# Rotary embedding on one core: stores moved from the ScalarE queue into the sync queue, and five TensorE tiles in place of three

## The chip, the core and the metric

The kernel runs on 1 core of one Trainium2 chip. The metric is device time in microseconds, the median of several executions. The engines in this text are TensorE (PE in the profile; PEld is its weight load), VectorE (DVE), ScalarE (ACT), GpSimd (POOL) and SyncE (SP), whose work here is to issue transfers. The 16 DMA engines of the core move all data between HBM and the on-chip memory SBUF; q1 is the queue fed by SP, q10 the one fed by ScalarE.

## The reference

```python
# x: (8, 2048, 8, 64) float32;  cos, sin: (2048, 32) float32
def reference(x, cos, sin):
    x1, x2 = x[..., :32], x[..., 32:]
    cos = cos[None, :, None, :]
    sin = sin[None, :, None, :]
    out1 = x1 * cos - x2 * sin
    out2 = x1 * sin + x2 * cos
    return np.concatenate([out1, out2], axis=-1)
```

Every element of x is read once (33.6 MB), and as much is written. The tables are small (0.26 MB each).

## The kernel before

**Slabs.** The sequence is cut into two groups of 1024 positions; in a group each of 128 partitions takes 8 consecutive positions. A slab is one batch and one group: 128 partitions x 4096 floats, 2 MB, 16 KB in one piece for each partition. There are 16 slabs, numbered 0 to 15; slabs 0 to 7 use the tables of group 0, slabs 8 to 15 those of group 1. A slab is loaded into a tile `xt` (nine of them, `NBUF`), rotated in place and stored from there, so load i + 9 has to wait until store i has landed.

**Rotation.** `rotate(i, lo, n)` works on a piece of a slab, in general a half (`UNIT`, 2048 floats per partition); the first half of slab 0 and the last half of slab 15 are cut once more. A piece has one of three kinds:

- kind A, the usual one: GpSimd makes `t2` in two instructions (L151), one half of the pairs times sin, the other times -sin; VectorE makes `t1 = x * cos` (L157) and then `x = t1 + t2` (L164).
- kind B: as A, but the add is done by TensorE: for each 512 columns a matmul of `t1` with the identity and one of `t2` with the identity add up in PSUM (L169, L170), and ScalarE copies the sum back to `xt` (L171).
- kind C: GpSimd does nothing; VectorE makes `x * cos` (L157) and `x * sin` (L174), TensorE adds them with the identity or its negative (L185, L186), and ScalarE copies (L189).

Before, three pieces are not of kind A: the second half of slab 5 (B), and both halves of slab 9 (C and B). `t2` has three buffers, and so has `t1s`, the SBUF tile of kinds B and C.

**Order.** The program is unrolled and handed to a scheduler; `keep(...)` fixes an instruction's place in its engine's program order, what isn't kept may be moved. Before, the DVE, ACT and store instructions are kept; loads and GpSimd's multiplications are not. The two halves of slab 0's first half therefore stand on GpSimd as sin, sin, -sin, -sin.

**Transfers.** Loads and tables are issued by SP (L82, L83, L89), stores by ScalarE (L196), where they stand in line with ScalarE's copies from PSUM and its table work (`prepare`). Store i - 2 is issued after slab i (`LAG = 2`), the last three after one another at the end. The nine first loads are at the head of SP's queue; load i + 6 comes after slab i.

Of the kernel before, what the change touches and what calls it, by code (L numbers as in the profile page):

```python
# [9 lines left out]
@with_exitstack  # L10
def kernel(
    ctx: ExitStack,
    tc: tile.TileContext,
    x: bass.AP,
    cos: bass.AP,
    sin: bass.AP,
    out: bass.AP,
):
    nc = tc.nc
    keep = tc.keep_in_program_order  # L20
    f32 = mybir.dt.float32
    PSUM = bass.MemoryType.PSUM

    B, S, H, D = x.shape
    Dh = D // 2
    P = 128
    HD = H * D
    R = S // P

    SL = 8  # L30
    n_half = R // SL
    SLAB = SL * HD
    UNIT = 4 * HD
    NBUF = 9
    C = 512

    xv = x.rearrange("b (g q r) h d -> b g q (r h d)", q=P, r=SL)
    ov = out.rearrange("b (g q r) h d -> b g q (r h d)", q=P, r=SL)
    cos_src = cos.rearrange("(g q r) d -> g q r d", q=P, r=SL)
    sin_src = sin.rearrange("(g q r) d -> g q r d", q=P, r=SL)  # L40

    const_pool = ctx.enter_context(tc.tile_pool(name="const", bufs=1))
    tab_pool = ctx.enter_context(tc.tile_pool(name="tab", bufs=1, space=PSUM))
    t1_pool = ctx.enter_context(tc.tile_pool(name="t1p", bufs=1, space=PSUM))
    o_pool = ctx.enter_context(tc.tile_pool(name="op", bufs=2, space=PSUM))
    t1s_pool = ctx.enter_context(tc.tile_pool(name="t1s", bufs=3))
    xpool = ctx.enter_context(tc.tile_pool(name="xpool", bufs=NBUF))
    t2_pool = ctx.enter_context(tc.tile_pool(name="t2p", bufs=3))

    eye = const_pool.tile([P, P], f32, tag="eye")  # L50
    neye = const_pool.tile([P, P], f32, tag="neye")
    TAB = [P, SL, Dh]
    cos_sb = [const_pool.tile(TAB, f32, tag=f"cb{g}", name=f"cos_sb{g}") for g in range(n_half)]
    sin_sb = [const_pool.tile(TAB, f32, tag=f"sb{g}", name=f"sin_sb{g}") for g in range(n_half)]
    nsin = [const_pool.tile(TAB, f32, tag=f"ns{g}", name=f"nsin{g}") for g in range(n_half)]
    cos_ps0 = tab_pool.tile(TAB, f32, tag="cp0")
    tab_ps1 = tab_pool.tile([P, 2, SL, Dh], f32, tag="tp1")
    cos_ps = [cos_ps0, tab_ps1[:, 0]]
    sin_ps = tab_ps1[:, 1]

    slabs = [(b, l) for l in range(n_half) for b in range(B)]
    last = len(slabs) - 1
    xts = {}

    def cuts(i):
        return [UNIT, UNIT] if i == 0 else [SLAB]

    def pieces(i):
        if i == 0:
            return [2 * HD, 2 * HD, UNIT]  # L70
        if i == last:
            return [UNIT, 2 * HD, 2 * HD]
        return [UNIT, UNIT]

    def spans(sizes):
        lo = 0
        for n in sizes:
            yield lo, n
            lo += n

    def tables(g):
        nc.sync.dma_start(out=cos_sb[g], in_=cos_src[g])  # L82
        nc.sync.dma_start(out=sin_sb[g], in_=sin_src[g])  # L83

    def load(i):
        b, l = slabs[i]
        xt = xpool.tile([P, SLAB], f32, tag="xt", name=f"xt{i}")
        for lo, n in spans(cuts(i)):
            nc.sync.dma_start(  # L89
                out=xt[:, lo : lo + n],  # L90
                in_=xv[b, l, :, lo : lo + n],
            )
            if i == 0 and lo == 0:
                tables(0)
        xts[i] = xt

    for i in range(NBUF):
        load(i)
        if i == 3:
            tables(1)  # L100

    nc.gpsimd.memset(eye, 0.0)  # L102
    nc.gpsimd.affine_select(
        out=eye,
        in_=eye,
        compare_op=mybir.AluOpType.not_equal,
        fill=1.0,
        base=0,
        pattern=[[-1, P]],
        channel_multiplier=1,  # L110
    )
    def prepare(g):
        keep(nc.scalar.mul(nsin[g], sin_sb[g], -1.0))  # L113
        if g == 0:
            keep(nc.vector.tensor_copy(cos_ps[g], cos_sb[g]))  # L115
        else:
            keep(nc.scalar.copy(cos_ps[g], cos_sb[g]))
            keep(nc.scalar.copy(sin_ps, sin_sb[g]))

    prepare(0)  # L120
    nc.scalar.mul(neye, eye, -1.0)

    def rep(a, n):
        return dataclasses.replace(a, ap=[a.ap[0][:], a.ap[1][:], [0, n], a.ap[-1][:]])

    kinds = {}
    kinds[(5, UNIT)] = "B"
    kinds[(9, 0)] = "C"
    kinds[(9, UNIT)] = "B"

    def rotate(i, lo, n):
        b, l = slabs[i]
        kind = kinds.get((i, lo), "A")
        xt = xts[i][:, lo : lo + n]
        r0 = lo // HD
        nr = n // HD
        xk = xt.rearrange("p (r k d) -> p r k d", r=nr, d=Dh)
        xu = xt.rearrange("p (g u d) -> p g u d", u=2, d=Dh)
        if kind == "A":
            t1 = t1_pool.tile([P, n], f32, tag="t1")  # L140
        else:
            t1 = t1s_pool.tile([P, n], f32, tag="t1s")
        if kind == "C":
            t2 = t1s_pool.tile([P, n], f32, tag="t1s")
        else:
            t2 = t2_pool.tile([P, n], f32, tag="t2")
        t1u = t1.rearrange("p (g u d) -> p g u d", u=2, d=Dh)
        t2u = t2.rearrange("p (g u d) -> p g u d", u=2, d=Dh)
        if kind != "C":
            for u, tab in ((1, sin_sb[l]), (0, nsin[l])):  # L150
                nc.gpsimd.tensor_mul(  # L151
                    out=t2u[:, :, u, :].rearrange("p (r h) d -> p r h d", h=H),
                    in0=xu[:, :, 1 - u, :].rearrange("p (r h) d -> p r h d", h=H),
                    in1=rep(tab[:, r0 : r0 + nr, :], H),
                )
        keep(
            nc.vector.tensor_mul(  # L157
                out=t1.rearrange("p (r k d) -> p r k d", r=nr, d=Dh),
                in0=xk,
                in1=rep(cos_ps[l][:, r0 : r0 + nr, :], 2 * H),  # L160
            )
        )
        if kind == "A":
            keep(nc.vector.tensor_add(out=xt, in0=t1, in1=t2))  # L164
        elif kind == "B":
            for j in range(n // C):
                o = o_pool.tile([P, C], f32, tag="o")
                cs = slice(j * C, (j + 1) * C)
                nc.tensor.matmul(o, eye, t1[:, cs], start=True, stop=False)  # L169
                nc.tensor.matmul(o, eye, t2[:, cs], start=False, stop=True)  # L170
                keep(nc.scalar.copy(xt[:, cs], o))  # L171
        else:
            keep(
                nc.vector.tensor_mul(  # L174
                    out=t2.rearrange("p (r k d) -> p r k d", r=nr, d=Dh),
                    in0=xk,
                    in1=rep(sin_ps[:, r0 : r0 + nr, :], 2 * H),
                )
            )
            G = C // Dh  # L180
            for u in range(2):
                for j in range(n // 2 // C):
                    o = o_pool.tile([P, C], f32, tag="o")
                    gs = slice(j * G, (j + 1) * G)
                    nc.tensor.matmul(o, eye, t1u[:, gs, u, :], start=True, stop=False)  # L185
                    nc.tensor.matmul(  # L186
                        o, eye if u else neye, t2u[:, gs, 1 - u, :], start=False, stop=True
                    )
                    keep(nc.scalar.copy(xu[:, gs, u, :], o.rearrange("p (g d) -> p g d", d=Dh)))  # L189

    LAG = 2

    def store(i, lo, n):
        b, l = slabs[i]
        keep(
            nc.scalar.dma_start(  # L196
                out=ov[b, l, :, lo : lo + n],
                in_=xts[i][:, lo : lo + n],
            )
        )  # L200

    for i in range(last + 1):
        if i == last:
            for k in range(i - LAG, i):
                store(k, 0, SLAB)
        for lo, n in spans(pieces(i)):
            rotate(i, lo, n)
            if i == last and lo == 0:
                store(i, 0, UNIT)
        if i == last:  # L210
            store(i, UNIT, UNIT)
        if LAG <= i < last:
            store(i - LAG, 0, SLAB)
        if i == 3:
            prepare(1)
        if i > LAG and i - LAG - 1 + NBUF <= last:
            load(i - LAG - 1 + NBUF)


# [28 lines left out]
```

## Time and profile before

| what | value |
|---|---|
| median of 5 runs | 165.54 us (164.69 to 166.45) |
| the profiled execution | 165.56 us |
| its span, first to last instruction | 163.7 us |
| DVE busy | 142.7 us (87%) |
| POOL busy | 143.2 us (87%) |
| PE busy | 26.1 us (16%) |
| ACT busy | 10.0 us (6%) |
| bytes moved | 67.65 MB, mean 413 GB/s over the span |
| q1 (loads), q10 (stores), share of 16 engines' span | 50.0%, 47.9% |
| transfers of SP | 15 loads of 2048 KB, 2 of 1024 KB, 4 tables of 128 KB |
| transfers of ScalarE | 15 stores of 2048 KB, 2 of 1024 KB |

The span is what the trace covers; the execution's time is 1.86 us longer. "Busy" leaves out the instructions that only issue a transfer, so SP shows no busy time. In the tables by stretch "DMA" is the mean busy share of the 16 DMA engines (1.00 is all of them; sums of rounded parts can be a little above), and GB/s is what they moved. In a timeline line the first number is the start, the second the time from the start of the first to the end of the last instruction merged into it, and the bracket gives the idle time of the engine just before, with what ended it.

### The profile page before, as it was taken

How to read it: one execution, taken by the hardware profiler on the slowest of the kernel's cores; microseconds unless marked ns; L12 is line 12 of the kernel's file. 1: busy time of each engine (PE TensorE's matmuls, PEld its weight loads, DVE VectorE, ACT ScalarE, POOL GpSimd, SP SyncE). 2: the span in 40 equal slices, each digit the busy share in tenths (PEclk: the TensorE clock that was granted, in tenths of full speed). 3: DMA queues.
4: the chain of work that ended last, by engine and by line, in shares of the span. 5: the costliest groups of instructions: out<-in, count | busy, mean ns of one | idle time of the engine just before them, and what ended most of it. 6: DMA issues, size and time to landing. Idle time of an engine off the chain costs nothing.

```text
span 163.7 us, 428 instructions
## 1 busy us (share of the span) xinstructions
PE 26.1 (16%) x48; PEld 10.5 (6%) x48; DVE 142.7 (87%) x67; ACT 10.0 (6%) x18; POOL 143.2 (87%) x72
## 2 busy tenths in 40 slices
PE   0000000000000004990000089991000000000000
PEld 0000000000000002430000034440000000000000
DVE  0449999999999999899999999999999999999910
ACT  3100000200000000130000002331000000000000
POOL 1399999999999999999999999899999999996000
PEclk9999999999999999997555558999755555555555
DMA  5999999999999999999999999999999999999993
GB/s 156 414 434 436 428 340 431 426 432 420 432 440 428 424 436 432 428 428 440 428 420 432 432 432 428 428 436 428 412 432 436 428 428 436 432 424 436 432 406 146
DMA packets 5474, 67.65 MB, mean 413 GB/s; under 512 B 608, under 2 KB 1120, under 8 KB 1120
## 3 DMA queue, kind: packets, MB, share of 16 engines
q1 hardware_dynamic: 3024, 34.08, 50.0%
q10 hardware_dynamic: 2448, 33.56, 47.9%
q14 instruction: 2, 0.02, 0.0%
HBM read 34.08 MB, written 33.55 MB: 413 GB/s over the span
## 4 chain that ended last, share of the span: by engine, by line
DVE 52%; POOL 30%; issue 9%; DMA 3%; SPq 0%; DVEq 0%; POOLq 0%
POOL t L151 30%; DVE t L157 27%; DVE xt L164 24%; DMA sin_sb<-in_sin_dram 3%; DVE t L174 1%; DVEq L164 0%; SPq L82 0%; SPq L89 0%; DVEq L157 0%; POOLq L151 0%
## 5 line engine op out<-in xcount | busy, mean ns | idle before, releaser
L151 POOL TENSOR_TENSOR t<-xt,sin_sb 128x1024 f32<-128x1024 f32 (+1 forms) x33 | 73.2, 2219 | 6.1 <-DMA sin_sb<-in_sin_dram 5.4
L151 POOL TENSOR_TENSOR t<-xt,nsin 128x1024 f32<-128x1024 f32 (+1 forms) x33 | 73.2, 2220 | 0.0
L164 DVE TENSOR_TENSOR xt<-t,t 128x2048 f32<-128x2048 f32 (+1 forms) x31 | 66.8, 2154 | 6.1 <-POOL t L151 3.0
L157 DVE TENSOR_TENSOR t<-xt,tab_ps 128x2048 f32<-128x2048 f32 (+1 forms) x17 | 36.8, 2168 | 0.5
L157 DVE TENSOR_TENSOR t<-xt,cos_ps 128x2048 f32<-128x2048 f32 (+1 forms) x17 | 36.8, 2168 | 0.5
L169 PE MATMUL o<-t,eye 128*128 128x512 f32 x16 | 9.9, 708 | 63.8 <-DVE t L157 63.8
L170 PE MATMUL o<-t,eye 128*128 128x512 f32 x16 | 9.1, 651 | 0.0
L185 PE MATMUL o<-t,eye 128*128 128x512 f32 x8 | 5.5, 780 | 21.3 <-DVE t L157 21.3
L169 PEld LDWEIGHTS o<-t,eye 128*128 128x128 f32 x16 | 3.5, 223 | 67.7 <-issue 67.7
L171 ACT COPY xt<-o 128x512 f32<-128x512 f32 x8 | 4.7, 585 | 44.5 <-PE o L170 44.5
L115 DVE COPY cos_ps<-cos_sb 128x256 f32<-128x256 f32 x1 | 0.4, 428 | 6.3 <-DMA cos_sb<-in_cos_dram 6.3
L189 ACT COPY xt<-o 128x512 f32<-128x512 f32 x4 | 2.3, 586 | 28.7 <-PE o L186 28.7
L170 PEld LDWEIGHTS o<-t,eye 128*128 128x128 f32 x16 | 3.5, 218 | 4.8 <-issue 4.8
L185 PEld LDWEIGHTS o<-t,eye 128*128 128x128 f32 x8 | 1.9, 258 | 24.1 <-issue 24.1
L186 PE MATMUL o<-t,neye 128*128 128x512 f32 x4 | 3.1, 867 | 0.1
L113 ACT ACTIVATE nsin<-sin_sb 128x256 f32<-128x256 f32 x2 | 0.8, 416 | 28.0 <-DMA sin_sb<-in_sin_dram 28.0
L174 DVE TENSOR_TENSOR t<-xt,tab_ps 128x2048 f32<-128x2048 f32 x1 | 2.3, 2282 | 0.0
L186 PE MATMUL o<-t,eye 128*128 128x512 f32 x4 | 2.0, 592 | 0.0
L113 ACT ACT_TABLE_LOAD x1 | 1.3, 1283 | 0.7 <-PEq L232 0.7
L186 PEld LDWEIGHTS o<-t,neye 128*128 128x128 f32 x4 | 0.9, 252 | 2.4 <-DVE t L174 1.6
L186 PEld LDWEIGHTS o<-t,eye 128*128 128x128 f32 x4 | 0.8, 190 | 1.0 <-issue 1.0
L102 POOL MEMSET eye<- 128x128 f32 x1 | 0.2, 204 | 0.3 <-POOLq L232 0.3
(8 smaller groups left out, 1.7 us busy)
## 6 DMA issues: line engine op xcount, KB each, us to landing
xt<-in_x_dram SPq DMA_DIRECT2D x15, 2048.0 KB, 24.7
out_dram<-xt ACTq DMA_DIRECT2D x15, 2048.0 KB, 16.4
xt<-in_x_dram SPq DMA_DIRECT2D x2, 1024.0 KB, 6.2
out_dram<-xt ACTq DMA_DIRECT2D x2, 1024.0 KB, 8.0
cos_sb<-in_cos_dram SPq DMA_DIRECT2D x2, 128.0 KB, 14.8
sin_sb<-in_sin_dram SPq DMA_DIRECT2D x2, 128.0 KB, 14.5
```

What stands on the lines that cost most here:

```text
L113: keep(nc.scalar.mul(nsin[g], sin_sb[g], -1.0))
L115: keep(nc.vector.tensor_copy(cos_ps[g], cos_sb[g]))
L151: nc.gpsimd.tensor_mul(out=t2u[:, :, u, :].rearrange("p (r h) d -> p r h d", h=H), in0=xu[:, :, 1 - u, :].rearrange("p (r h) d -> p r h d" ...
L157: nc.vector.tensor_mul(out=t1.rearrange("p (r k d) -> p r k d", r=nr, d=Dh), in0=xk, in1=rep(cos_ps[l][:, r0 : r0 + nr, :], 2 * H),)
L164: keep(nc.vector.tensor_add(out=xt, in0=t1, in1=t2))
L169: nc.tensor.matmul(o, eye, t1[:, cs], start=True, stop=False)
L170: nc.tensor.matmul(o, eye, t2[:, cs], start=False, stop=True)
L171: keep(nc.scalar.copy(xt[:, cs], o))
L174: nc.vector.tensor_mul(out=t2.rearrange("p (r k d) -> p r k d", r=nr, d=Dh), in0=xk, in1=rep(sin_ps[:, r0 : r0 + nr, :], 2 * H),)
L185: nc.tensor.matmul(o, eye, t1u[:, gs, u, :], start=True, stop=False)
L186: nc.tensor.matmul(o, eye if u else neye, t2u[:, gs, 1 - u, :], start=False, stop=True)
L189: keep(nc.scalar.copy(xu[:, gs, u, :], o.rearrange("p (g d) -> p g d", d=Dh)))
```

## The change

- Stores are issued by SP (`nc.sync`) in place of ScalarE, each right after its own slab (store i after slab i; `LAG` is gone), and load i + 8 comes directly behind store i. All loads, tables and stores are kept in program order, so SP's order is: the nine first loads with the tables, store 0, store 1, load 9, store 2, load 10, ..., store 7, load 15, store 8, store 9, ..., store 15 in two halves. Load i + 8 waits for the landing of store i - 1, whose `xt` it takes.
- ScalarE issues no transfers; it keeps its table work and the copies from PSUM.
- Five pieces in place of three go over TensorE: the second half of slab 4 (B), and both halves of slabs 8 and 11 (C and B each).
- GpSimd's multiplications are kept in program order: sin, -sin for each piece.

```diff
     def tables(g):
-        nc.sync.dma_start(out=cos_sb[g], in_=cos_src[g])
-        nc.sync.dma_start(out=sin_sb[g], in_=sin_src[g])
+        keep(nc.sync.dma_start(out=cos_sb[g], in_=cos_src[g]))
+        keep(nc.sync.dma_start(out=sin_sb[g], in_=sin_src[g]))
 
     def load(i):
         b, l = slabs[i]
         xt = xpool.tile([P, SLAB], f32, tag="xt", name=f"xt{i}")
         for lo, n in spans(cuts(i)):
-            nc.sync.dma_start(
-                out=xt[:, lo : lo + n],
-                in_=xv[b, l, :, lo : lo + n],
+            keep(
+                nc.sync.dma_start(
+                    out=xt[:, lo : lo + n],
+                    in_=xv[b, l, :, lo : lo + n],
+                )
             )
...
     kinds = {}
-    kinds[(5, UNIT)] = "B"
-    kinds[(9, 0)] = "C"
-    kinds[(9, UNIT)] = "B"
+    kinds[(4, UNIT)] = "B"
+    for i in (8, 11):
+        kinds |= {(i, 0): "C", (i, UNIT): "B"}
...
             for u, tab in ((1, sin_sb[l]), (0, nsin[l])):
-                nc.gpsimd.tensor_mul(
-                    out=t2u[:, :, u, :].rearrange("p (r h) d -> p r h d", h=H),
-                    in0=xu[:, :, 1 - u, :].rearrange("p (r h) d -> p r h d", h=H),
-                    in1=rep(tab[:, r0 : r0 + nr, :], H),
+                keep(
+                    nc.gpsimd.tensor_mul(
+                        out=t2u[:, :, u, :].rearrange("p (r h) d -> p r h d", h=H),
+                        in0=xu[:, :, 1 - u, :].rearrange("p (r h) d -> p r h d", h=H),
+                        in1=rep(tab[:, r0 : r0 + nr, :], H),
+                    )
                 )
...
-    LAG = 2
-
     def store(i, lo, n):
         b, l = slabs[i]
         keep(
-            nc.scalar.dma_start(
+            nc.sync.dma_start(
                 out=ov[b, l, :, lo : lo + n],
                 in_=xts[i][:, lo : lo + n],
             )
         )
 
     for i in range(last + 1):
-        if i == last:
-            for k in range(i - LAG, i):
-                store(k, 0, SLAB)
         for lo, n in spans(pieces(i)):
             rotate(i, lo, n)
             if i == last and lo == 0:
                 store(i, 0, UNIT)
         if i == last:
             store(i, UNIT, UNIT)
-        if LAG <= i < last:
-            store(i - LAG, 0, SLAB)
+        else:
+            store(i, 0, SLAB)
         if i == 3:
             prepare(1)
-        if i > LAG and i - LAG - 1 + NBUF <= last:
-            load(i - LAG - 1 + NBUF)
+        if i >= 1 and i - 1 + NBUF <= last:
+            load(i - 1 + NBUF)
```

## The prediction

> **What bounds the kernel now.** I read the page first (engines, slices, queues), then the table of busy time by stretch, then the DMA queues inside single stretches, then the timelines of VectorE and ScalarE, and last the waits of the sync queue.
>
> ```profile
> span 163.7 us, 428 instructions
> PE 26.1 (16%) x48; PEld 10.5 (6%) x48; DVE 142.7 (87%) x67; ACT 10.0 (6%) x18; POOL 143.2 (87%) x72
> GB/s 156 414 434 436 428 340 431 426 432 420 432 440 428 424 436 432 428 428 440 428 420 432 432 432 428 428 436 428 412 432 436 428 428 436 432 424 436 432 406 146
> DMA packets 5474, 67.65 MB, mean 413 GB/s; under 512 B 608, under 2 KB 1120, under 8 KB 1120
> q1 hardware_dynamic: 3024, 34.08, 50.0%
> q10 hardware_dynamic: 2448, 33.56, 47.9%
> ```
>
> Two engines are busy 87% of the span, which looks like a compute bound. But every slice but the ends and one shows 412 to 440 GB/s. The stretches (after the times: PE, PEld, DVE, ACT, POOL, granted clock, DMA share, GB/s) say more:
>
> ```profile
> 1.10:4.50 3.40, 0.00 (x0) 0.00 (x0) 0.00 (x0) 0.92 (x1) 0.20 (x1) 1.00 0.82 246
> 4.50:19.00 14.50, 0.00 (x0) 0.00 (x0) 9.95 (x8) 0.61 (x2) 12.31 (x8) 1.00 1.02 427
> 19.00:23.50 4.50, 0.00 (x0) 0.00 (x0) 4.40 (x2) 0.00 (x0) 4.50 (x3) 1.00 1.01 353
> 48.00:122.00 74.00, 26.13 (x48) 10.53 (x48) 71.69 (x32) 7.02 (x12) 73.30 (x33) 0.80 1.01 430
> 122.00:156.00 34.00, 0.00 (x0) 0.00 (x0) 32.82 (x17) 0.00 (x0) 27.85 (x15) 0.50 1.00 430
> 156.00:160.00 4.00, 0.00 (x0) 0.00 (x0) 0.07 (x1) 0.00 (x0) 0.00 (x0) 0.50 1.00 422
> 160.00:163.70 3.70, 0.00 (x0) 0.00 (x0) 0.00 (x0) 0.00 (x0) 0.00 (x0) 0.50 0.27 113
> ```
>
> From 4.5 to 160 us the 16 DMA engines are never idle: the share is 1.00 or more whether the queues carry loads, stores or both. 67.65 MB at 430 GB/s is 157.3 us; the rest of the span is the 1.1 us before the first packet, a soft start (0.18 x 3.4 = 0.6 us of idle engines), one stretch of 353 GB/s at full share (19 to 23.5), some small packets, and a tail in which the engines end unevenly. The DMA engines are the bound, with compute close behind: the last VectorE add ends at 154.84 + 1.23 = 156.07, when 1.00 x 4.0 + 0.27 x 3.7 = 5.0 us of DMA work is still to do, and the last piece (1 MB) is only 2.4 us of it. So the last add could have come about 2.6 us later for nothing, and gains nothing by coming earlier.
>
> ```profile
> 10.40 1.23 DVE L164 TENSOR_TENSOR xt<-t,t 128x1024 f32<-128x1024 f32 x1 [2.45 <-POOL t L151]
> 16.65 2.29 DVE L164 TENSOR_TENSOR xt<-t,t 128x2048 f32<-128x2048 f32 x1
> 66.42 2.29 DVE L164 TENSOR_TENSOR xt<-t,t 128x2048 f32<-128x2048 f32 x1 [0.55 <-POOL t L151]
> 154.84 1.23 DVE L164 TENSOR_TENSOR xt<-t,t 128x1024 f32<-128x1024 f32 x1
> 73.45 1.87 ACTq L196 DMA_DIRECT2D out_dram<-xt  x4
> SPq L89 <- DMA out_dram<-xt: 91.1, 7, 31.8
> ```
>
> The fifth line shows what ScalarE's double duty does: four stores leave together at 73.45, behind the copies of the tile at (5, UNIT). It looks costly, but in that time (53 to 76.8 us) the load queue alone moved 431 GB/s. The sixth: SP waits 91 us in seven waits for stores that must free a slot; that is the pacing of a full pipe.
>
> **The change part by part.** The sum is made on the profiled execution, 165.56 us (span 163.7, 1.86 around it); the median of the runs is 165.54, so nothing is shifted.
>
> *Stores from ScalarE to SP.* 17 issues of 0.34 us (5.8 us) leave ScalarE and go to SP, which had 21 of 0.33 to 0.65. Neither engine's time matters: SP's waits alone are over 150 us. What matters is order. SP now runs store i, load i+8, store i+1, ... and load i+8 waits until store i-1 has landed; behind that wait stand store i+1 and everything later. For the DMA engines to stay full, enough must be queued during each such wait. One slab is 2.097 MB, 4.9 us at 430 GB/s. Loads 0 to 8 and the four tables (19.4 MB) take until about 48 us. VectorE finishes slab i at about 19 + 9.4 i (first slab at 18.97, a mul and an add at 2.32 + 2.40 = 4.72 per half slab), so stores 0 and 1 (19 and 28 us) are queued by then. Store 0 ends at about 53; load 9 is then issued with only store 1 ahead, 4.9 us of cover. From there each load is issued with a load and a store ahead, 9.8 us, and store i+1 (ready by 19 + 9.4(i+1), due at about 53 + 9.8 i) is long waiting: 24 us ahead at store 2, more later.
>
> What must the cover hide? Landing and wake-up: not shown singly; between 0 and 1.0 (last store issued 156.1, landed 6.6 later at 162.7, span's end 163.7); I take 0.5. Issue to first packet: the store issued at 18.97 has no packet in 19 to 23.3 and 71% of the engines in 23.3 to 24, 4.4 us; the load issued at 84.37 has none in 84.4 to 87.7, 57% after 87.8, 3.4 us. These queue behind the other queue's packets, so they are upper bounds; the low bound is 0.4 (first load issued 0.74, first packet 1.1). At load 9: 4.9 - 0.5 - 4.4 = 0, worst 4.9 - 1.0 - 4.4 = -0.5. Gap 0 to 0.5, taken 0.3. The later six loads keep over 4 us: nothing. Without the second slab of cover each would pay as load 9 does, some 2 us in all.
>
> The Trainium skill, "DMA: Bandwidth & Descriptors", section "Latency and other measured facts", gives about 0.6 us to the first byte of such a DMA, and says of the fixed cost of about 2 us that the receipt from HBM is most of it. The trace's 3.4 and 4.4 us contradict the first, at least on busy engines. By the page load 9 has 4.9 - 2 - 0.6 = 2.3 us to spare and the 0.3 goes, an estimate of 164.8 for the whole; by the rows it stays.
>
> *The slow stretch.* From 19 to 23.5 us 353 GB/s instead of 430 costs 4.5 x 77/430 = 0.8 us. It begins when the second queue gets its first transfer and ends when that queue's packets come; later starts of the same queue (32, 41, 77, 115 us) show nothing like it, and the first queue's own start is soft too. After the change there is no second queue. Bounds: 0 (it belongs to the first write, and comes at 48 us instead) to -0.8; the row it is nearest to is a queue's first use, so -0.8.
>
> *Turning round inside one queue.* Loads and stores now alternate in one ring: load 8 to store 0, then store 1, load 9, store 2, ... load 15, store 8: 15 turns. The trace has no such turn. Nearest rows: transfer after transfer in one direction in one queue, 431 GB/s (53 to 76.8, loads) and 430 (122 to 156, stores), and two queues mixed by packet, 430 (48 to 122): nothing each. The other end: a cold start, 0.6 us (above), x 15 = 9.0. A gain has a reason against it, the share being already 1.00. I take 0, since the mixed stretch turns far more often.
>
> *Loads.* x9 lands at about 62 us and is needed after 9 slabs, at about 92; x15 lands when 16 loads, 8 stores and the tables are through (50.9 MB, about 120) and is needed near 139. Nothing; the cover is 18 us.
>
> *Five tiles and GpSimd's order.* GpSimd's halves now finish t of the first piece at 9.1 instead of 10.40; VectorE is then held by GpSimd's third piece (16.09 + 0.05 instead of 16.65), so 0.5 is left. Tiles at (4,UNIT), (8,both), (11,both): adds fall from 31 to 29 (-4.6), one more mul on VectorE (+2.2), two muls of 2.3 fewer on GpSimd. The tile at (4,UNIT) comes when GpSimd leads by only some 1.3 us, so VectorE waits there about 1.0 where it waited 0.55 at 66.42. VectorE's end: 156.07 - 0.5 - 2.4 + 0.4 = 153.6. TensorE goes from 24 to 40 matmul pairs and ScalarE from 12 to 20 copies; a tile's four copies pass every 1.72 us, 7 us a tile, and slab 8 (two tiles) is ready near 104, due at 122; slab 11 near 129, due at 136. All of it lies under the DMA engines: 0. If that cover were gone (an end later than about 158), each us would cost one.
>
> Sum: 165.56 + 0.3 - 0.8 + 0 = **165.1 us**.
>
> **The rivals.** (1) *Turns cost.* Some 15 refills between 48 and 122 us, in the queue. For it: all of the read-write mixing in the trace is between two rings. Against it: no row has a stall between two transfers. It decides from (1.66 + 0.5)/15 = 0.14 us a turn; at half the cold start, 0.3, it adds 4.5: 169.6. (2) *Compute sets the end.* With the stores issued in order, a stall of over 4 us on VectorE or GpSimd shows at once; for it, 87% of two engines; against, the 5 us of DMA work left behind the last add today, and 2.5 more. A stall of 6 would give about 167. (3) *The tail evens out.* From 160 to the landing at 162.7 only 1.0 of 2.7 us is used: 1.7 is lost to the one or two engines that end last. Half of it back, with the 0.8 and no gap at load 9, gives 165.56 - 0.8 - 0.85 = 163.9, all of it 163.1. (4) *The slow stretch and an exposed load 9 stay:* 165.56 + 0.5 = 166.1; inside the forecast's own case.
>
> **How the numbers follow.** A measurement of this kernel can tell about 1% (1.66 us) from no change. Forecast with (4): within 1%, 0.65. Turns: 0.18, slower. Compute end: 0.05, slower. Tail: 0.12, faster. So faster 0.12, same 0.65, slower 0.23. The forecast's own range is 164.3 to 166.5; the 8 in 10 reach from 163.8 (half the tail and a little more) to 168.3 (turns of some 0.2), and leave out about 0.07 below and 0.11 above.
>
> **What would show it.** Right: one queue with 67.6 MB; 1.00 and about 430 GB/s in every stretch from 4.5 to 160, through 48 to 122 as well; no dip near 20 us; VectorE's last add near 153.6 and a span near 163.2. Wrong: a share under 0.97 or a lower rate where loads and stores alternate (turns), a dip just after 53 us (load 9), a dip that moved to 48 us (first write), idle DMA engines after 140 us (compute).

## The result and the profile after

The changed kernel took 166.36 us (median of 44 runs, 165.11 to 167.35), the kernel before 165.58 (79 runs): 1.0045 times as long, 95% interval 1.0032 to 1.0058. The forecast was 165.1, a gain of 0.5 us; what came is a loss of about 0.75. It is small, but clear of the noise, and on the other side. The time lies inside the stated range. Ratios below are against runs of the kernel before on the same chip. (Of the two kernels that alternate half loads and half stores, seven of twelve runs took 171.6 to 179.8 us, for a reason that stays open, and are not in the ratios.)

The page of the kernel after, lines that answer to those shown of before:

```profile
span 164.3 us, 496 instructions
PE 42.0 (26%) x80; PEld 17.0 (10%) x80; DVE 140.0 (85%) x66; ACT 14.7 (9%) x26; POOL 138.8 (84%) x70
GB/s 171 413 429 435 427 423 427 427 431 431 423 427 435 431 411 427 427 427 435 407 433 429 431 423 423 435 427 431 423 419 443 431 431 423 439 431 431 413 431 66
q1 hardware_dynamic: 5472, 67.64, 97.5%
```

All bytes are in one queue, the slice of 340 GB/s is gone, and VectorE and GpSimd have less to do. Judged by busy time alone this kernel should be faster. Its table by stretch (after the times: PE, PEld, DVE, ACT, POOL, granted clock, DMA share, GB/s):

```profile
19.00:23.50 4.50, 0.00 (x0) 0.00 (x0) 4.36 (x3) 0.00 (x0) 4.50 (x3) 1.00 0.98 410
48.00:122.00 74.00, 36.78 (x69) 15.04 (x70) 71.25 (x32) 9.37 (x16) 71.15 (x32) 0.77 1.01 426
122.00:156.00 34.00, 5.21 (x13) 1.99 (x11) 30.19 (x16) 2.34 (x4) 25.61 (x14) 0.65 1.00 430
160.00:164.30 4.30, 0.00 (x0) 0.00 (x0) 0.00 (x0) 0.00 (x0) 0.00 (x0) 0.50 0.20 86
```

Two rows matter. From 48 to 122 us, where loads and stores alternate, the 16 DMA engines are full (1.01) and yet move 426 GB/s instead of 430. And after 160 us they are used at 0.20, where before it was 0.27 of 3.7 us: they end less evenly. The same table cut at single transfers (load 9, store 2, then load 13, store 6):

```profile
58.90:63.80 4.90, 3.72 (x9) 1.33 (x7) 4.76 (x3) 1.76 (x3) 4.90 (x3) 1.00 1.01 411
63.80:68.70 4.90, 0.00 (x0) 0.00 (x0) 4.76 (x3) 0.00 (x0) 4.90 (x4) 0.87 1.01 431
99.00:104.30 5.30, 3.59 (x9) 1.32 (x7) 5.14 (x4) 1.75 (x3) 5.24 (x4) 1.00 1.00 417
104.30:109.40 5.10, 0.00 (x0) 0.00 (x0) 5.00 (x3) 0.00 (x0) 5.10 (x3) 0.56 1.01 434
```

The load behind a store is the slow one; the store behind a load is not. These are two of the clearest loads: of the other five, load 11 shows 416 GB/s (78.9 to 83.9 us) and the rest 425 to 429. A full share at a lower rate means that packets take longer, not that engines wait for work. The trace also marks, for each transfer, when each of the 16 DMA engines has landed its part. In the kernel after, the last mark comes 0.4 us behind the median one for store 0 (53.9 us), and 2.35 us for load 14 (114.7 us), and it stays there to the last piece: some engines are held up more than others, and here they don't catch up. Before, the last piece had 1.44 us of this. The same marks give the price of a load: from the last mark of one transfer to the last mark of the next, the seven loads behind a store took 4.88 to 5.68 us, 36.2 in all, and the seven stores behind those loads 4.85 to 4.88, 34.1 in all. That is 0.3 us a load. Summed over engines the packets' time is nearly the same in both kernels (160.5 us per engine before, 160.4 after): after has lost the slow stretch and has the long packets in its place.

### The profile page after: what moved, and what is told of

The parts are those of the page before. It is cut to its first block, busy times and chain, and to the rows that moved or that the text cites. A ratio compares the mean times of both kernels' runs of the same rounds, so it can differ in the third digit from the quotient of the medians.

```text
span 164.3 us, 496 instructions
## 1 busy us (share of the span) xinstructions
PE 42.0 (26%) x80; PEld 17.0 (10%) x80; DVE 140.0 (85%) x66; ACT 14.7 (9%) x26; POOL 138.8 (84%) x70
## 5 line engine op out<-in xcount | busy, mean ns | idle before, releaser
L155 POOL TENSOR_TENSOR t<-xt,sin_sb 128x1024 f32<-128x1024 f32 (+1 forms) x32 | 70.8, 2212 | 11.1 <-DMA sin_sb<-in_sin_dram 5.4
L155 POOL TENSOR_TENSOR t<-xt,nsin 128x1024 f32<-128x1024 f32 (+1 forms) x32 | 70.8, 2214 | 0.0
L169 DVE TENSOR_TENSOR xt<-t,t 128x2048 f32<-128x2048 f32 (+1 forms) x29 | 62.2, 2145 | 6.4 <-POOL t L155 3.8
L174 PE MATMUL o<-t,eye 128*128 128x512 f32 x24 | 13.3, 637 | 53.9 <-DVE t L162 53.9
L190 PE MATMUL o<-t,eye 128*128 128x512 f32 x16 | 11.3, 796 | 31.2 <-DVE t L162 31.2
L175 PE MATMUL o<-t,eye 128*128 128x512 f32 x24 | 13.0, 624 | 0.0
L174 PEld LDWEIGHTS o<-t,eye 128*128 128x128 f32 x24 | 4.8, 206 | 59.5 <-issue 59.5
L176 ACT COPY xt<-o 128x512 f32<-128x512 f32 x12 | 7.0, 585 | 44.2 <-PE o L175 44.2
L194 ACT COPY xt<-o 128x512 f32<-128x512 f32 x8 | 4.7, 585 | 46.2 <-PE o L191 46.2
L190 PEld LDWEIGHTS o<-t,eye 128*128 128x128 f32 x16 | 3.9, 257 | 36.8 <-issue 36.8
L191 PE MATMUL o<-t,neye 128*128 128x512 f32 x8 | 6.2, 873 | 0.1
L175 PEld LDWEIGHTS o<-t,eye 128*128 128x128 f32 x24 | 4.9, 202 | 6.3 <-issue 6.3
L179 DVE TENSOR_TENSOR t<-xt,tab_ps 128x2048 f32<-128x2048 f32 x2 | 4.6, 2281 | 0.0
L191 PE MATMUL o<-t,eye 128*128 128x512 f32 x8 | 4.1, 592 | 0.0
L191 PEld LDWEIGHTS o<-t,neye 128*128 128x128 f32 x8 | 2.0, 275 | 4.8 <-DVE t L179 3.3
L191 PEld LDWEIGHTS o<-t,eye 128*128 128x128 f32 x8 | 1.5, 190 | 1.9 <-issue 1.9
```

Of the source, the lines that this page charges most:

```text
L155: nc.gpsimd.tensor_mul(out=t2u[:, :, u, :].rearrange("p (r h) d -> p r h d", h=H), in0=xu[:, :, 1 - u, :].rearrange("p (r h) d -> p r h d" ...
L179: nc.vector.tensor_mul(out=t2.rearrange("p (r k d) -> p r k d", r=nr, d=Dh), in0=xk, in1=rep(sin_ps[:, r0 : r0 + nr, :], 2 * H),)
L191: nc.tensor.matmul(o, eye if u else neye, t2u[:, gs, 1 - u, :], start=False, stop=True)
```

## The experiments

Theory T: a change of direction inside one queue stalls the DMA engines. Rivals: R1, one queue as such, however seldom it turns; R2, the five tiles and GpSimd's order; R4, the other engines' traffic; R5, loads issued too late. "After" is the changed kernel.

**1. Stores back on ScalarE's queue, all else as after.**

```diff
-            nc.sync.dma_start(
+            nc.scalar.dma_start(
                 out=ov[b, l, :, lo : lo + n],
```

> The kernel after, with the stores issued by ScalarE again; tiles, order on GpSimd and order of the loads stay. Theory T (a change of direction inside one queue stalls the DMA engines, some more than others): the 15 turns are gone, the slow stretch near 20 us is back (0.8 us), so 165.2 to 165.8. Rival R1 (one queue as such is the cause, whatever the number of turns): the same as T. Rival R2 (the five tiles and the new order on GpSimd are the cause, by their SBUF traffic or their timing): stays at 166.3 or above.

Measured: 164.81 us, 0.9969 (0.9951 to 0.9987). Faster than T expected; R2 falls. Its rows against those of after:

```profile
19.00:23.50 4.50, 0.00 (x0) 0.00 (x0) 4.36 (x3) 0.00 (x0) 4.50 (x3) 1.00 1.00 350
48.00:122.00 74.00, 36.38 (x67) 14.79 (x68) 71.20 (x32) 9.78 (x18) 71.22 (x32) 0.77 1.01 432
```

The slow stretch is back (350 against 410), and the mixed one runs at 432 instead of 426.

**2. Only the transfers of after** (tiles and GpSimd's order of before).

```diff
-    kinds[(4, UNIT)] = "B"
-    for i in (8, 11):
-        kinds |= {(i, 0): "C", (i, UNIT): "B"}
+    kinds[(5, UNIT)] = "B"
+    kinds[(9, 0)] = "C"
+    kinds[(9, UNIT)] = "B"
...
-                keep(
-                    nc.gpsimd.tensor_mul(
+                nc.gpsimd.tensor_mul(
```

> The kernel after with the tiles of before ((5,UNIT), both halves of 9) and GpSimd's multiplications not kept in order: only the transfers are changed. T and R1: 166.3, as after. R2: below before, about 164.8, since the slow stretch is gone and nothing is added.

Measured: 166.79 us, 1.0067 (1.0042 to 1.0093). The loss sits in the transfers.

**3. The compute side alone**: the kernel before with the five tiles and GpSimd's halves in order (the reverse of the edit above, on before).

> The kernel before with the five tiles and GpSimd's halves in program order; loads, stores and queues of before. Stores on ScalarE with all else of after gave 0.9969 of before. If that gain comes from VectorE's earlier end: about 165.0 here (0.997). If it comes from the order of stores and loads (store i right after slab i, with fewer restarts of an empty queue): 165.4 to 165.7 (1.000).

Measured: 166.99 us, 1.0088 (1.0053 to 1.0123): neither. Its stretches from 122 us and ScalarE's timeline say why:

```profile
127.00:129.00 2.00, 1.02 (x3) 0.19 (x1) 1.85 (x1) 0.59 (x1) 2.00 (x2) 1.00 0.20 82
128.06 0.59 ACT L173 COPY xt<-o 128x512 f32<-128x512 f32 x1 [1.13 <-PE o L172]
128.12 20.57 ACTq L198 DMA_DIRECT2D out_dram<-xt  x7
```

With tiles at 8 and 11, the stores in ScalarE's line stand behind the eight copies of slab 11 until 128.12. By then loads and stores are through, and the DMA engines stand idle for 0.80 x 2 = 1.6 us. This is the cost that taking the stores out of ScalarE's old order avoids; before, the stores that left together at 73.45 were covered by loads. Less those 1.6 us it would be 0.999, so a gain of the tiles by themselves isn't shown.

**4. Fewer turns, same transfers.** SP's loads are grouped behind several stores:

```diff
-        if i >= 1 and i - 1 + NBUF <= last:
-            load(i - 1 + NBUF)
+        for j in runs.get(i, ()):
+            load(j)
```

with `runs = {6: range(9, 16)}` (3 turns) and `{3: range(9, 13), 6: range(13, 16)}` (5 turns).

> The kernel after with SP's order loads 0 to 8, stores 0 to 6, loads 9 to 15, stores 7 to 15: 3 turns in place of 15, one queue. T: four fifths of the turns' stalls (0.85 us in the mean over the engines) and of the unevenness that they leave at the end go: 164.8 to 165.5, a last landing near 162. R1 and R2: 166.3. If loads 9 and 10, which land at about 88 and 93 us here, come late for GpSimd, a VectorE wait near 90 us would show it.

Measured: 165.46 us, 1.001 (0.9984 to 1.0035): faster than after, but the late loads held up the end. GpSimd stands 3.73 us until load 9 has landed. With that it loses its lead, and its next wait reaches VectorE: it starts again at 102.44, where the profile names no releaser, but TensorE's last matmul on slab 8, which reads one of the three `t2` buffers, ends at 101.28 + 1.02 = 102.30 (with 5 turns the profile names this wait, 3.16 us until 102.36). VectorE waits 4.33 us for GpSimd then, and the last add ends at 157.65 + 1.23 = 158.88:

```profile
88.71 2.34 POOL L155 TENSOR_TENSOR t<-xt,sin_sb 128x1024 f32<-128x1024 f32 x1 [3.73 <-DMA xt<-in_x_dram]
101.28 1.02 PE L175 MATMUL o<-t,eye 128*128 128x512 f32 x2
102.44 2.32 POOL L155 TENSOR_TENSOR t<-xt,sin_sb 128x1024 f32<-128x1024 f32 x1 [4.44 <-issue]
107.07 2.29 DVE L169 TENSOR_TENSOR xt<-t,t 128x2048 f32<-128x2048 f32 x1 [4.33 <-POOL t L155]
157.65 1.23 DVE L169 TENSOR_TENSOR xt<-t,t 128x1024 f32<-128x1024 f32 x1
158.00:159.00 1.00, 0.00 (x0) 0.00 (x0) 0.88 (x1) 0.00 (x0) 0.00 (x0) 0.50 0.16 66
159.00:160.00 1.00, 0.00 (x0) 0.00 (x0) 0.00 (x0) 0.00 (x0) 0.00 (x0) 0.50 0.32 131
```

0.84 + 0.68 = 1.5 us of the DMA engines are lost there, waiting for the last piece.

> One queue, order loads 0 to 8, stores 0 to 3, loads 9 to 12, stores 4 to 6, loads 13 to 15, stores 7 to 15: 5 turns. The loads of 9 to 12 land near 73 to 88 us, so GpSimd shouldn't wait for them, and VectorE's last add should come near 152 to 153, not at 158.9 as with 3 turns. T: 163.7 to 164.5 (the 165.5 with 3 turns less the 1.6 us in which the DMA engines stood idle for the last piece, plus two turns of about 0.1). If the 3 turns' time was not held up by that idle time: 165.5.

Measured: 164.71 us, 0.9954 (0.9933 to 0.9974), 0.2 us above T's range, and faster than both kernels, with one queue:

```profile
48.00:122.00 74.00, 36.96 (x65) 14.88 (x66) 70.58 (x32) 8.79 (x15) 70.29 (x32) 0.77 1.01 430
```

So R1 falls: one queue is as good as two if it turns seldom.

**5. Halves, alternating or not** (29 turns; and 15 turns with as many transfers).

```diff
+                store(i, 0, UNIT)
+                load_half(j, 0)
+                store(i, UNIT, UNIT)
+                load_half(j, UNIT)
```

> The kernel after with stores 1 to 7 and loads 9 to 15 cut in halves that alternate: 29 turns in place of 15, and 14 transfers more. T: another 0.8 us in the mean and as much again on the last engine: 167.1 to 168.0. R1 and R2: 166.3 to 166.5.

> The kernel after with stores 1 to 7 and loads 9 to 15 in halves that do not alternate (both halves of the store, then both of the load): 15 turns as after, and the 14 transfers more of the alternating kernel. T (turns are what costs): 166.2 to 166.6, steady from run to run. Rival: the smaller transfers cost, and this is as slow and as unsteady as the alternating halves (167 and up).

Measured: alternating, 1.011 (1.0068 to 1.0152), from two of six runs, 166.75 and 167.56. Together: 166.92 us, 1.0081 (1.0046 to 1.0115), all eight within 166.6 to 167.3, above T's range and below the rival's. The intervals overlap, and the smaller transfers seem to cost something by themselves, so the ratios do not settle it.

**6. Nothing but transfers.** `rotate` and `prepare` return at once, in after, in the kernel with 5 turns, with 3, with 29, and in the kernel of experiment 1.

> The transfers of after, in its order, with all arithmetic left out (each slab is stored as it was loaded). T: the stall belongs to the DMA engines alone, so the long packets at loads 9 to 15 are there without any work on the other engines, and the time is that of after: 165.9 to 166.5. Rival R4 (the stall needs the other engines' SBUF traffic): no long packets, 164.3 to 164.7, the same as the copy with 5 turns.

> The transfers of the kernel with 5 turns, with all arithmetic left out. T: 164.4 to 164.8, 1.2 to 1.8 below the copy with 15 turns. R4: the same as the copy with 15 turns.

> The transfers of the kernel with 3 turns (one from stores to loads), with all arithmetic left out, so that no late piece holds up the end. T2: at or a little below the copy with 5 turns (0.9968): 0.992 to 0.997. If only the queue's depth matters: the same as the copy with 5 turns, and so not told apart by this run alone.

> Loads on SP's queue, stores on ScalarE's, with all arithmetic left out: no turn inside a queue, though loads and stores mix from 9 us on. T2: 0.990 to 0.998, a slow stretch at the first store included. Rival (loads and stores in flight together are slow whatever the queue): 1.005 and above.

> The transfers of the kernel with alternating halves (29 turns, 14 from stores to loads), with all arithmetic left out. T: above the copy with 15 turns (1.007): 1.012 or more, with long packets at every half load. Rival: as the copy with 15 turns, and what the alternating halves cost more came from the work on the other engines.

Measured against before: 15 turns 1.0071 (1.0043 to 1.0099), 5 turns 0.9968 (0.9933 to 1.0003), 3 turns 0.9934 (0.9898 to 0.9971), two queues 0.9934 (0.9908 to 0.996), 29 turns 1.0124 (1.0063 to 1.0185, from three of six runs). The copies with 15 and 5 turns took 166.78 and 165.38 us, both above T's times by 0.3 and 0.6; their difference is as T has it. The interval for 29 turns takes in the 1.0071 for 15, so it doesn't show that still more turns cost more. The rows from 48 to 122 us, for 15 turns and for two queues (the numbers: ACT, POOL, granted clock, DMA share, GB/s):

```profile
48.00:122.00 74.00, 0.00 (x0) 0.00 (x0) 1.00 1.01 426
48.00:122.00 74.00, 0.00 (x0) 0.00 (x0) 1.00 1.01 432
```

426 and 432 again, with no compute engine at work (429 with 5 turns, 430 with 3): R4 falls. And leaving all arithmetic out gains nothing with 15 turns (1.0071 against 1.0045 with it) or with 5 (0.9968 against 0.9954): these two kernels are bound by the DMA engines alone.

**7. Nine turns, three ways.** `runs = {1: (9, 10), 3: (11, 12), 5: (13, 14), 6: (15,)}`, then `7: (15,)` in place of the last, then `{2: (9, 10), 4: (11, 12), 6: (13, 14), 7: (15,)}`.

> One queue, nine turns: stores 0, 1, loads 9, 10, stores 2, 3, loads 11, 12, stores 4, 5, loads 13, 14, stores 6, 7, load 15 - no: load 15 directly after store 6 - so four turns from stores to loads, where after has seven and the kernel with 5 turns has two. The traces put nearly all long packets of after at the beginning of loads 9 to 15. T: between the two, 165.2 to 165.8 (1.000, from 1.0045 and 0.9954). If the number of such turns doesn't matter: as after or as the kernel with 5 turns.

Measured: 170.49 us, 1.0305 (1.025 to 1.036). Load 15 waited for store 6, the only transfer in the queue:

```profile
113.00:117.00 4.00, 3.94 (x9) 1.83 (x9) 4.00 (x3) 0.94 (x2) 4.00 (x3) 0.83 0.31 78
```

That is an empty queue: 0.69 x 4 = 2.8 us in this row alone. So the price of turns can't be read from this order, and the next one avoids the empty queue.

> One queue: stores 0, 1, loads 9, 10, stores 2, 3, loads 11, 12, stores 4, 5, loads 13, 14, stores 6, 7, load 15, stores 8 to 15: four turns from stores to loads (seven in after, two with 5 turns in all), and no load waits with an empty queue ahead of it as load 15 did in the first kernel with nine. T: 0.998 to 1.002 of before, no idle DMA engines before 160 us.

Measured: 167.74 us, 1.014 (1.0094 to 1.0186), against T: nine turns cost more than fifteen, with a full share and 417 GB/s:

```profile
48.00:122.00 74.00, 35.96 (x66) 14.61 (x67) 71.26 (x32) 9.37 (x16) 71.17 (x32) 0.77 1.01 417
```

Here each load is issued with one transfer ahead of it, in after with two (load 9 apart). So the number of turns is not all.

> One queue: stores 0 to 2, loads 9, 10, stores 3, 4, loads 11, 12, stores 5, 6, loads 13, 14, store 7, load 15, stores 8 to 15: nine turns, four from stores to loads, as in the kernel that gave 1.014, but with two to four transfers queued ahead of each load in place of one. Theory T2 (turns cost, and a load issued with one transfer ahead costs more): 0.996 to 1.003. Rival (nine turns in pairs are bad in themselves, the queue's depth doesn't matter): 1.010 to 1.018.

Measured: 165.89 us, 1.002 (0.9994 to 1.0047), 429 GB/s in that row. With two to four transfers ahead, nine turns lie between five and fifteen, though the interval overlaps that of after.

**8. A deeper queue, as many turns**: `runs = {i: (i + 7,) for i in range(2, 9)}`.

> After with every load one place later: store i, then load i + 7. Still 15 turns, seven of them from stores to loads, but load i + 7 waits for store i - 2, so three transfers (14.7 us) are ahead of it in place of two. T: the turns cost what they cost in after, 1.003 to 1.006. Rival R5 (in after the loads are issued too late, and the long packets are that): 0.995, as with 5 turns.

Measured: 166.51 us, 1.0074 (1.0049 to 1.0099), a little above T and far from R5's 0.995. R5 falls: three transfers ahead do not help at 15 turns.

**9. The slow stretch near 20 us.** Group 0's tables through ScalarE's queue in the kernel before; then group 1's in the kernel of experiment 1. The second edit (the first has the two queues the other way round):

```diff
-        keep(nc.sync.dma_start(out=cos_sb[g], in_=cos_src[g]))
+        q = nc.sync if g == 0 else nc.scalar
+        keep(q.dma_start(out=cos_sb[g], in_=cos_src[g]))
```

> The kernel before with the two tables of group 0 loaded through ScalarE's queue at the start, so that this queue is in use from 1 us on. If the 353 GB/s between 19 and 23.5 us belong to a queue's first use: gone there, 164.8 (0.995). If they belong to the first store: still there, 165.5.

> After with the stores on ScalarE's queue again (0.9969) and the tables of group 1 loaded through that queue at the start, ahead of its other work, so that the queue is in use from 1 us on while SP's first transfers stay as they are. If the 353 GB/s near 20 us belong to the queue's first use: gone, 164.0 to 164.4 (0.992 to 0.994), the fastest of all; if to the first store: as without the warming, 164.8.

Measured: 165.78 us, 1.0021 (0.9998 to 1.0044), with 417 GB/s in the stretch, and 164.37 us, 0.9936 (0.9915 to 0.9957), with 364 there. In the first the total tells nothing: the tables came later, VectorE's last add ended at 158.86, and the DMA engines stood idle at the end, which hid any gain. Its rows (lines 1 and 2 below) lose only 0.2 us against 430 GB/s, though its first store was issued at 21.28. The second (line 3) kept its early start, had the queue in use from 1 us on, and was still slow when the first store came. And in the copy with two queues, whose first store is issued at 9.38, the slow stretch is there and not at 19 to 23.5 (lines 4 and 5):

```profile
19.00:23.50 4.50, 0.00 (x0) 0.00 (x0) 4.47 (x2) 0.00 (x0) 4.50 (x3) 1.00 1.01 417
23.50:26.00 2.50, 0.00 (x0) 0.00 (x0) 2.37 (x2) 0.00 (x0) 2.50 (x2) 1.00 1.11 415
19.00:23.50 4.50, 0.00 (x0) 0.00 (x0) 4.36 (x3) 0.00 (x0) 4.50 (x3) 1.00 1.01 364
9.00:15.00 6.00, 0.00 (x0) 0.00 (x0) 1.00 0.99 358
19.00:23.50 4.50, 0.00 (x0) 0.00 (x0) 1.00 1.00 430
```

So the stretch moves with the first store, and a queue in use since 1 us can still have it (364); why the first kernel almost escapes it is not known.

The second is the fastest of all kernels that compute, but its interval overlaps that of experiment 1 (0.9951 to 0.9987), so what the warming brings is not settled.

## Why the prediction was wrong

**The bound: right.** The DMA engines bind; the copies of experiment 6 show it better than the profile did. VectorE's last add was put at 153.6; it ended at 152.33 + 1.23 = 153.56, and gained nothing by it, as predicted. The warning that an end much later than 158 costs time held with 3 turns and with the early tables (158.88 and 158.86, 1.5 us and more of idle engines).

**The slow stretch: near in size, wrong in reason.** 0.8 us was taken off, as if the stretch would run at 430 GB/s. It runs at 410 in place of 353, which is 4.5 x 57/430 = 0.6. It was put down to the second queue's first use, and experiment 9 shows it (364) in a queue long in use. What remains is that it comes with the first store on a second queue, in all such kernels here but one.

**Load 9's gap, 0.3: nothing.** The share is 1.01 in 58.9 to 63.8, though load 9 was issued at 54.01 with one store ahead. The 3.4 and 4.4 us from issue to first packet were upper bounds, as the prediction said, and an empty queue answers faster. With 3 turns the last piece was issued at about 158.9, and the engines are 0.32 busy in 159 to 160 and 1.03 after, so some 0.8 us. In the first kernel with nine turns load 15 was issued at 115.63, 0.4 us after the last packet of store 6, and its first packet came at 116.59, 1.0 us after the issue. Load 9 by itself does not decide between these figures: 4.9 - 0.4 - 4.4 would leave no gap either. The Trainium skill, "DMA: Bandwidth & Descriptors", section "Latency and other measured facts", has about 0.6 to the first byte; the 0.8 and 1.0 here are nearer to it than to the rows that were taken.

**Turning round inside one queue: the step that failed.** It was bounded by 0 and 9.0 us and taken as 0, "since the mixed stretch turns far more often". That row was two queues; it says nothing about turns in one. The rival "Turns cost" had the right place, though it thought of refills: the runs show full engines (1.01) and packets that take longer. Three pairs give the price. After against experiment 1: 1.0045 - 0.9969 is 1.26 us, and the slow stretch that only the latter has is 0.6 more (350 against 410 GB/s over 4.5 us): 1.9/15 = 0.13 us a turn. Fifteen against five turns: 1.0045 - 0.9954 is 1.5 us for ten turns, 0.15 each; in the copies 1.7 us by the ratios and 1.4 by the medians, 0.14 to 0.17 each. The traces put the cost on the load behind a store, of which after has seven: some 0.3 us each. With these two terms the prediction's sum is 165.6 - 0.6 + 1.9 = 166.9, and 0.5 below that is measured. That the time still lies inside the stated range is luck: those 0.5 us were not in the sum either. Experiment 1 shows those 0.5 us as the gain (0.9969) of all that is left of the change when the stores stay on ScalarE's queue; whether they come from the tiles or from storing each slab at once, with the engines ending more evenly, was not separated.

The Trainium skill, same page, section "Issuing engines are not separate DMA queues", says that starting transfers from several engines only saves issue time. Here SP and ScalarE had issue time to spare, and one queue against two still made 0.76% (experiment 1 against after): the measurement decides.

**What stays open.** Why a load behind a store meets long packets is not shown; they fall on some engines more than on others (the marks above), in some loads and not in others (load 15 of after has hardly any). With one transfer ahead of each load (1.014) the second load of a pair, which follows a load, is hit as well: loads 10, 12 and 14 took 5.6 to 5.7 us from mark to mark. The runs show that few turns and two or more transfers ahead go together with a fast kernel, not what happens in the engine.

**A version that beats both.** One queue with 5 turns (0.9954), stores on ScalarE's queue in after's order (0.9969), and the latter with group 1's tables ahead (0.9936).

## What to carry to other kernels

When the DMA engines are full in every row, look at the rate beside the share: a full share at a lower rate is time too, and it is neither compute nor waiting. In this case merging two queues that mix loads and stores paid only where the merged order kept long runs in one direction, with two or more transfers queued ahead of each load; a row of two mixed queues is no price for turns in one. And an end that has slack should be watched: here 2 to 5 us of it hid every change in the compute engines, until an experiment used it up.

## What the runs showed of the hardware

Alternating 2 MB loads and stores in one queue cost about 0.3 us for each load that follows a store, with full DMA engines; it is there with no compute engine at work as well (426 against 432 GB/s). The stalls fall unevenly on the 16 engines, and in after they were not made up: the last engine ended 2.35 us behind the median one, in experiment 1 0.6 us. A load issued with nothing queued ahead left the engines idle for about 3 us.
